# GLA loop of a hybrid diffusion step: early forward output, a buffer for the w_ada blocks, decay two slots ahead, output norm folded into the weights

## The chip, the cores and the metric

The kernel runs on one core of one Trainium2 chip. The metric is the device time of one execution in microseconds (us); lower is better. The engines are PE (TensorE: matmuls; its weight loads are listed apart as PEld), DVE (VectorE), ACT (ScalarE), POOL (GpSimd) and SP (SyncE, which here issues most DMAs).

## The reference

One inference step of two layers on 256 context tokens and 1024 latent tokens with 1024 channels. Layer 0 is gated linear attention (GLA), layer 1 softmax attention. Each layer normalises its input, modulates it with shift and scale vectors that come from `silu(c) @ w_ada + b_ada`, mixes tokens, multiplies by `silu(gate)`, projects with an output matrix and adds the result, times a gate vector, to the input. What matters here is the GLA layer, per head, cut to its core:

```
def step(S, inp):                      # one chunk of tokens
    qe, ke = qi * exp(b), ki * exp(-b)     # b: running sum of the log decay
    a = where(mask, qe @ ke.T, 0)
    o = a @ vi + qe @ S                    # within the chunk + from the state
    S = exp(b_last) * S + (ki * exp(b_last - b)).T @ vi

o_f = scan(forwards);  o_b = scan(backwards)
o = rms_norm(o_f + flip(o_b), onorm)       # per head, 256 values
y = (o * silu(gate)) @ w_out
```

There are 4 heads with 128 key and 256 value channels. The log decay is `log_sigmoid((h @ wa1) @ wa2 + ba) / 16`, one for each direction.

## The kernel before, in words

Matmuls that need more than half precision are made of three: each operand is split into a high and a low half-precision part (`mm3`, L113). Weights are therefore prepared first: `stage` (L129) loads 1 MB into a tile `wst`, of which there are two for everybody, takes the largest absolute value (four reductions, L135) and derives a power of two from it (`pow2`, L72, with a matmul at L77 that spreads the maximum over the partitions). `fill` (L143) then writes the high part with ACT (L150) and the low part with DVE (L151); `split_ahead` (L154) does the same for the attention weights and stores them to memory.

**The GLA loop** (`gla`, L585) has 50 slots: five passes over the ten tiles of 128 tokens. Pass h handles head h in one direction (forwards for even h, backwards for odd h) and, in the same slots, finishes head h-1 in the opposite direction. In before, a slot does this, in program order:

- `combine` (L536) finishes head h-1 on tile i: three products are summed in one PSUM bank (L548): scores times values (`at`, `v`), queries times the state of the first direction (`Sa`), queries times the state of the second direction (`Sc`). ACT sums the squares (L551), DVE and POOL take the root (L107, L109), and DVE multiplies by the row factor and the norm vector `onorm` (L554).
- `decayed` (L456) turns the decay of this slot into `en`, `ep` and so into `ke` and `qe` by a matmul with a triangle matrix (L461) into the bank `cs`.
- `decay` (L434) prepares the decay of the next slot: a matmul into bank `z` (L437), three ACT steps (L442 to L444), DVE (L446, L447), and the split into `ghi` on POOL (L451) and `glo` on DVE (L452).
- `value_gate` (L414) projects value and gate of the tile (the many matmuls of L118) and applies silu to the gate.
- `intra` (L474) transposes the keys into bank `kt` (L479), copies them out (`ks`, L481), makes the scores in bank `A` (L484), masks them (L487) and adds the two directions (`at`, L489).
- `gated` (L557) multiplies output and gate (L559) and stores the tile.
- `filler` (L1153) does work of other stages in fixed slots: in even slots from 4 on, `gemv` (L221) loads a 1 MB block of `w_ada` into a `wst` tile (L227) and multiplies it with the conditioning vectors (16 small matmul instructions, L231); `mod_sum` adds it up a slot later; other slots split weights ahead (`AHEAD`, L39) or fill the output weights (`WO`, L37).
- `outer` (L492) makes the tile's share of the state in bank `U` (L500, L503), ACT copies one half out (`u`, L505), and `scan` (L509) advances the state with DVE (`Wa`, `Wc`, L527) and POOL (`Sa`, `Sc`, L521, L523).

The PSUM has eight banks; in the loop they are two `mm` (projections, `gemv`, `mod_sum`), `z` (decay, and the spreading matmul of `pow2`), `cs`, `A`, `kt`, `U` and `o`.

**The order of the work** isn't written out by hand. The Tile framework is called with a simulated timeline (L44): while the program is built it places each ready instruction on its engine, those earlier in the program first, and adds the waits for tiles and banks. What comes out is one fixed order for each engine and each DMA queue; at run time an instruction that has to wait holds back those behind it.

After the loop `gla_out` multiplies by the output weights (`wo`), and layer 1 follows.

Of the kernel before, what the change touches and what calls it, by code (L numbers as in the profile page):

```python
# [7 lines left out]
F16 = mybir.dt.float16  # L8
F32 = mybir.dt.float32
I32 = mybir.dt.int32  # L10
AF = mybir.ActivationFunctionType
# [36 lines left out]
class K:  # L48
# [92 lines left out]


    def fill(self, w, j, ap):  # L143
# [59 lines left out]
    def cond_vectors(self, rows, brow):  # L203
# [14 lines left out]
        self.modT = [self.t(cp, [P, 16, 2], F32, f"modT{l}") for l in range(2)]  # L218


    def gemv(self, l, b, tag="mm", first=None):  # L221
        nc = self.nc
        src = self.I["w_ada"][l, :, b * 256 : b * 256 + 256].rearrange("(k p) n -> p k n", p=P)
        to = self.t(self.wst, [P, KT, 256], F32, "wst") if first is None else first
        h = KT if first is None else KT // 2
        for j in range(0, KT, h):
            nc.sync.dma_start(to[:, j : j + h], src[:, j : j + h])  # L227
        ps = self.bank(tag)
        for k in range(KT):
            j = k % 4  # L230
            nc.tensor.matmul(  # L231
                ps[32 * j : 32 * j + 32, 0:256], self.cst[:, k, :], to[:, k, :],
                start=k < 4, stop=k >= 4, tile_position=(0, 32 * j), skip_group_check=True,
            )
        m = self.t(self.ew, [P, 256], F32, "mod") if first is None else self.t(self.p1, [P, 256], F32, "mod", bufs=4)
        nc.scalar.copy(m, ps[:, 0:256])
        return l, b, m
# [79 lines left out]
    def gla_consts(self):  # L317
        nc, I = self.nc, self.I
        load = nc.gpsimd.dma_start
        self.ia = self.io = 0  # L320
        self.r = self.t(self.gcp, [98, T], F16, "r")
        self.wa2 = self.t(self.gcp, [98, 2, GQ], F16, "wa2")
        self.cum = self.t(self.gcp, [P, 2, 130], F16, "cum")
        load(self.cum, I["k_cum"])
        self.mask = self.t(self.gcp, [P, 2, P], I32, "mask")
        load(self.mask, I["k_mask"])
        self.onorm = self.t(self.gcp, [P, DV], F32, "onorm")
        load(self.onorm, I["gla_onorm"].to_broadcast([P, DV]))
# [85 lines left out]
    def value_gate(self, h, i, w):  # L414
# [3 lines left out]
        if h < GH:  # L418
            v = self.t(self.tl, [P, DV], F32, f"v{i}")
            self.nc.scalar.activation(v, ps[:, 0:DV], AF.Copy, scale=self.inv_v[h])  # L420
            self.v[h][i] = v
# [12 lines left out]
    def decay(self, h, i):  # L434
# [39 lines left out]
    def intra(self, i, st):  # L474
        nc = self.nc
        ke, qe = st["ke"], st["qe"]
        kt = self.bank("kt")[:, 0 : 2 * P].rearrange("p (d k) -> p d k", d=2)
        for d in range(2):
            nc.tensor.transpose(kt[:, d, :], ke[:, d, :], self.ident)  # L479
        ks = self.t(self.ew, [P, 2, P], F32, "ks")  # L480
        nc.vector.tensor_copy(ks, kt)  # L481
        ap = self.bank("A")[:, 0 : 2 * P].rearrange("p (d k) -> p d k", d=2)
        for d in range(2):
# [3 lines left out]
        nc.vector.copy_predicated(am, self.mask, ap)  # L487
        at = self.t(self.tl, [P, P], F32, f"at{i}")
        nc.gpsimd.tensor_tensor(at, am[:, 0, :], am[:, 1, :], ALU.add)  # L489
# [19 lines left out]
    def scan(self, h, i, d, prev, u, eb, tag):  # L509
        nc = self.nc  # L510
        if prev is None and i < NTP:
# [4 lines left out]
            return None, w  # L516
        s = self.t(self.tl, [P, DV], F32, f"Sa{i}") if tag == "a" else self.t(self.ew, [P, DV], F32, "Sc")
        if prev is None:
# [16 lines left out]

    def combine(self, h, i, c, st, prev):  # L536
        nc = self.nc
        a = 1 - c
        sc, wc = self.scan(h, i, c, prev, st["u"], st["eb"], "c")
        o = self.bank("o" if h < GH - 1 else ("o", "A", "U", "kt")[self.io % 4])[:, 0:DV]  # L540
        self.io += 1
        terms = [(st["at"], self.v[h][i])]
        if st["S"] is not None:
            terms.append((st["qe"][:, a, :], st["S"]))
        if sc is not None:
            terms.append((st["qe"][:, c, :], sc))
        for j, (x, y) in enumerate(terms):
            nc.tensor.matmul(o, x, y, start=j == 0, stop=j == len(terms) - 1)  # L548
        junk = self.t(self.ew, [P, DV], F16, "junk", bufs=1)
        ssq = self.t(self.sm, [P, 1], F32, "ossq")  # L550
        nc.scalar.activation(junk, o, AF.Square, accum_out=ssq)  # L551
        r = self.rstd(ssq, DV, "ors")
        og = self.t(self.ew, [P, DV], F32, "og", bufs=3)
        nc.vector.scalar_tensor_tensor(og, o, r, self.onorm, ALU.mult, ALU.mult)  # L554
        return og, {"W": wc, "eb": st["eb"]}

    def gated(self, h, i, og, g):  # L557
        nc = self.nc
        nc.vector.tensor_tensor(og, og, g, ALU.mult)  # L559
        nc.scalar.dma_start(self.og_d[i, :, h * DV : h * DV + DV], og)  # L560

# [23 lines left out]
    def gla(self, wq, w, filler):  # L585
        asc = list(range(NTP, NT)) + list(range(NTP))
        st = [[None] * NT for _ in range(GH)]
        g = {0: self.decay(0, asc[0])}
        for h in range(GH + 1):
            order = asc if h % 2 == 0 else asc[::-1]  # L590
            a, ends = (0, (NT - 1, NTP - 1)) if h % 2 == 0 else (1, (NTP, 0))
# [6 lines left out]
            for n, i in enumerate(order):  # L598
                slot = h * NT + n
                if i in starts:  # L600
                    prev = cprev = None
                if h > 0:
                    og, cprev = self.combine(h - 1, i, a, st[h - 1][i], cprev)
                if h < GH:
                    s = st[h][i] = self.decayed(h, i, g.pop(slot))
                h2, n2 = divmod(slot + 1, NT)
                if h2 < GH:
                    g[slot + 1] = self.decay(h2, (asc if h2 % 2 == 0 else asc[::-1])[n2])
# [7 lines left out]
                filler(slot)  # L616
                if h < GH:
                    self.outer(h, i, a, s, prev, i in ends)
                    prev = s
                    if i < NTP and i in ends:  # L620
                        self.final_state(h, a, prev)
# [414 lines left out]
def emit(ctx, tc, I, O, dbg=None, stop=None):  # L1036
# [26 lines left out]
    with ExitStack() as c:  # L1063
# [4 lines left out]
        k.ps = k.pool("ps2", 1, PSUM, c)  # L1068
        k.p2_bank = "z"
        banks = ("z", "cs", "A", "kt", "U", "o")  # L1070
        k.gla_init()
        with ExitStack() as c1:
# [24 lines left out]
            for j, b in enumerate((4, 5, 6, 7, 0, 1, 2, 3)):  # L1097
# [8 lines left out]
                to = to.bitcast(F32).rearrange("p (k n) -> p k n", n=256)  # L1106
                parts.append(k.gemv(0, b, ("A", "kt", "U", "o")[j % 4], to))
                if j == 3:
# [41 lines left out]
        queue = [(0, b) for b in (8, 9, 10, 11)] + [(1, b) for b in (4, 5, 6, 7, 0, 1, 2, 3, 8, 9, 10, 11)]  # L1150
        wo, part, prep = [], [], []

        def filler(slot):  # L1153
            if part:
                k.mod_sum([part.pop()])
            if queue and slot >= 4 and slot % 2 == 0:
                part.append(k.gemv(*queue.pop(0)))
            if cols and slot in AHEAD:
                with tc.issue_after(first):
                    k.split_ahead(*cols.pop(0))  # L1160
            if slot in WO:
                b = WO.index(slot)
                if b % 2 == 0:
                    wo.append(k.wtile(b))
                k.fill(wo[-1], b % 2, I["gla_w_out"][0][:, 256 * b : 256 * b + 256])
            if slot == 43:
# [133 lines left out]
```

## Time and profile before

| | us |
|---|---|
| Median of 3 runs | 1375.09 (1372.32 to 1375.16) |
| Profiled execution | 1372.38 |
| its span, first to last instruction | 1370.6 |
| PE busy in the span | 1253.7 |
| DVE busy | 945.3 |
| ACT busy | 653.0 |
| POOL busy | 378.1 |

The GLA loop runs from about 105 to 625 us of the span. A matmul's own duration overlaps that of the next, so the distance between two starts is what it costs PE; the granted PE clock is 1.00 at full speed. In rows of instructions stand the start, the duration, the engine, the line, the operation, the tile written and those read, the shapes, and in square brackets how long the engine stood idle before and what released it. In lists of waits stand the total, the number and the longest.

### The profile page before, as it was taken

To read this page: it belongs to the slowest core of one execution; us is meant where nothing else is said; L and a number is where in the kernel's file an instruction comes from. 1 tells how busy PE (TensorE), PEld (TensorE's weight loads), DVE (VectorE), ACT (ScalarE), POOL (GpSimd) and SP (SyncE) were. 2 spreads that over 40 slices of the span, in tenths; PEclk is the share of its full clock that TensorE was granted. 3 is DMA by queue.
4 is the path that set the end of the run, shared out by engine and by line. 5 is a ranking of instruction groups with operands and counts; after the bars stand their busy time and mean duration, and the time that the engine had idled before them with its cause. 6 is when DMAs were issued, how large, how long until landed. Compare 5 with 4: busy or idle time off the path is not lost. (4 is left out here: it accounts for less than half of the span.)

```text
span 1370.6 us, 21814 instructions
## 1 busy us (share of the span) xinstructions
PE 1253.7 (91%) x7646; PEld 762.0 (56%) x7646; DVE 945.3 (69%) x2148; ACT 653.0 (48%) x1621; POOL 378.1 (28%) x607
## 2 busy tenths in 40 slices
PE   4788899989979998997999998999999989998998
PEld 2346564645545554773444445676765766765443
DVE  2787568765767668876565468888767788875652
ACT  2566345544546445752233356555556455563110
POOL 1233112322311123330122356344335443330000
PEclk9899899999989998998999999999999999999999
DMA  9511545244445435147643446756947666694342
GB/s 324 200 62 43 188 155 170 93 138 143 135 135 185 154 112 168 54 167 212 151 150 108 162 112 139 145 120 142 191 95 166 129 156 139 122 211 139 132 144 93
DMA packets 343486, 198.18 MB, mean 145 GB/s; under 512 B 233598, under 2 KB 331374, under 8 KB 341840
## 3 DMA queue, kind: packets, MB, share of 16 engines
q1 hardware_dynamic: 297312, 158.64, 43.4%
q10 hardware_dynamic: 45728, 37.25, 8.2%
q0 software_dynamic: 336, 0.90, 0.3%
q8 instruction: 60, 0.98, 0.3%
q14 instruction: 50, 0.41, 0.1%
HBM read 103.39 MB, written 37.24 MB: 103 GB/s over the span
## 5 line engine op out<-in xcount | busy, mean ns | idle before, releaser
L118 PE MATMUL mm<-whi,hT_hi 128*128 128x512 f16 (+1 forms) x560 | 198.0, 354 | 0.6 <-ACT gx L918 0.6
L118 PE MATMUL mm<-wlo,hT_hi 128*128 128x512 f16 (+1 forms) x560 | 197.6, 353 | 0.0
L118 PE MATMUL mm<-whi,hT_lo 128*128 128x512 f16 (+1 forms) x560 | 197.1, 352 | 0.0
L118 PEld LDWEIGHTS <-hT_hi 128*128 128x128 f16 x1280 | 125.6, 99 | 111.9 <-issue 6.9
L118 PEld LDWEIGHTS <-whi 128*128 128x128 f16 x1328 | 132.2, 100 | 92.3 <-issue 21.9
L118 PE MATMUL mm<-hT_hi,whi 128*128 128x256 f16 (+1 forms) x512 | 156.8, 309 | 3.5 <-POOL hT_hi L313 2.9
L906 POOL TENSOR_SCALAR phi<-p,srec 128x1280 f16<-128x1280 f32 (+1 forms) x80 | 106.1, 1326 | 191.9 <-DVE srec L901 179.9
L118 PE MATMUL mm<-hT_lo,whi 128*128 128x256 f16 (+1 forms) x512 | 157.0, 307 | 0.4 <-DVE hT_lo L314 0.4
L118 PE MATMUL mm<-hT_hi,wlo 128*128 128x256 f16 (+1 forms) x512 | 156.9, 307 | 0.0
L907 DVE SCALAR_TENSOR_TENSOR plo<-p,srec,phi 128x1280 f16<-128x1280 f32 (+1 forms) x80 | 106.8, 1335 | 40.0 <-POOL phi L906 34.2
L891 PE MATMUL S<-kTh,wst 128*128 128x512 f16 (+1 forms) x416 | 114.4, 338 | 4.2 <-ACT p L899 2.1
L894 DVE TENSOR_REDUCE smx<-S 128x1 f32<-128x1280 f32 (+1 forms) x80 | 101.2, 1267 | 8.6 <-PE S L891 8.6
L118 PE MATMUL mm<-PTh,vh 128*128 128x256 f16 x336 | 91.8, 273 | 13.0 <-DMA PTh<-phi 12.4
L899 ACT ACTIVATE p<-S,snb,sexp 128x1280 f32<-128x1280 f32 (+1 forms) x80 | 99.3, 1241 | 4.2 <-ACT snb L896 0.4
L118 PE MATMUL mm<-PTl,vh 128*128 128x256 f16 x336 | 91.8, 273 | 7.5 <-DMA PTl<-plo 7.4
L118 PEld LDWEIGHTS <-hT_lo 128*128 128x128 f16 x640 | 63.1, 99 | 60.9 <-DVE hT_lo L314 3.1
L135 DVE TENSOR_REDUCE wmx<-wst 128x1 f32<-128x512 f32 x120 | 74.5, 676 | 30.5 <-DMA wst<-in_att_w_in 13.4
L118 PE MATMUL mm<-PTh,vl 128*128 128x256 f16 x336 | 91.9, 273 | 0.0
L891 PEld LDWEIGHTS <-wst 128*128 128x128 f16 x624 | 61.0, 98 | 54.4 <-issue 3.0
L118 PEld LDWEIGHTS <-wlo 128*128 128x128 f16 x640 | 63.6, 99 | 37.2 <-issue 4.7
L118 PEld LDWEIGHTS <-vh 128*128 128x128 f16 x672 | 65.8, 98 | 26.7 <-issue 9.1
L891 PE MATMUL S<-kTl,wst 128*128 128x512 f16 (+1 forms) x208 | 70.3, 338 | 0.0
(336 smaller groups left out, 2712.3 us busy)
## 6 DMA issues: line engine op xcount, KB each, us to landing
wst<-in_w_ada SPq DMA_DIRECT2D x16, 1024.0 KB, 5.9
wst<-in_gla_w_in SPq DMA_DIRECT2D x12, 1024.0 KB
wst<-in_att_w_in SPq DMA_DIRECT2D x10, 1024.0 KB, 6.3
og_d<-og ACTq DMA_DIRECT2D x80, 128.0 KB, 2.1
x_d<-xr ACTq DMA_DIRECT2D x10, 512.0 KB, 5.2
wst<-og_d SPq DMA_DIRECT2D x5, 1024.0 KB, 4.9
xr<-x_d SPq DMA_DIRECT2D x10, 512.0 KB, 6.8
out<-xr ACTq DMA_DIRECT2D x10, 512.0 KB, 2.6
```

Of the source, the lines that this page charges most:

```text
L118: self.nc.tensor.matmul(out, a, b, start=k == 0 and j == 0, stop=k == n - 1 and j == 2)
L135: nc.vector.tensor_reduce(mx[:, j : j + 1], st[:, 2 * j : 2 * j + 2, :], AX.XY, ALU.max, apply_absolute_value=True)
L891: nc.tensor.matmul(S[:, a : a + n], x, y, start=m == 0, stop=m == 2)
L894: nc.vector.tensor_reduce(mx, S, AX.X, ALU.max)
L899: nc.scalar.activation(p, S, AF.Exp, scale=self.sexp, bias=nb, accum_out=den)
L906: nc.gpsimd.tensor_scalar(hi, p, r, 2.0 ** 14, ALU.mult, ALU.mult)
L907: nc.vector.scalar_tensor_tensor(lo, p, r2, hi, ALU.mult, ALU.subtract)
```

## The change

Five edits, all in the GLA loop.

- **Forward output early.** `combine` is split. `local` runs in the slot after the tile's own first pass: it sums the first two products in one half of bank `o`, and ACT copies them to a tile `oa`. `combine`, a pass later, makes only the third product, in the other half of the bank, and DVE adds `oa`. The tiles `v`, `at` and `Sa`, one for each token tile before, are now two in turn. `combine` also moves from the head of the slot to behind `intra`.
- **Banks.** `kt` and `A` become the halves of one bank `kA`; the bank that this frees, `p2`, takes the spreading matmul of `pow2`, which was in `z`.
- **w_ada blocks.** The load (`ada_load`) is called in odd slots from 1 on, into a buffer of its own; the matmuls (`gemv`) in the even slot after it.
- **Decay** is called two slots ahead rather than one; `ghi` and `glo` get three buffers each.
- **Norm in the weights.** `onorm` is multiplied into the rows of `gla_w_out` while these are split (`fill_out` in place of `fill`); `gated` multiplies output, row factor and gate in one instruction.

The diff, cut to its core:

```diff
+    def fill_out(self, w, j, ap):
+        nc = self.nc
+        st = self.t(self.wst, [P, KT, 256], F32, "wst")
+        nc.sync.dma_start(st, ap.rearrange("(k p) n -> p k n", p=P))
...
+        o2 = self.onorm.unsqueeze(1).to_broadcast([P, 2, 2])
+        nc.vector.tensor_tensor(mx, mx, o2, ALU.mult)
+        m = self.t(self.small, [P, 1], F32, "wm1")
+        nc.vector.tensor_reduce(m, mx, AX.XY, ALU.max, apply_absolute_value=True)
+        s, w[2][j] = self.pow2(m)
+        so = self.t(self.small, [P, 2], F32, "wso")
+        nc.vector.tensor_scalar(so, self.onorm, s, None, ALU.mult)
...
+                nc.scalar.activation(hi, par[:, q, :, b, :], AF.Copy, scale=so[:, b : b + 1])
+                nc.vector.scalar_tensor_tensor(lo, par[:, q, :, b, :], so[:, b : b + 1], hi, ALU.mult, ALU.subtract)
...
+    def ada_load(self, l, b, to, h=KT):
         src = self.I["w_ada"][l, :, b * 256 : b * 256 + 256].rearrange("(k p) n -> p k n", p=P)
-        to = self.t(self.wst, [P, KT, 256], F32, "wst") if first is None else first
...
+            self.nc.sync.dma_start(to[:, j : j + h], src[:, j : j + h])
+        return l, b, to
...
-            v = self.t(self.tl, [P, DV], F32, f"v{i}")
+            v = self.t(self.tl, [P, DV], F32, "v", bufs=2)
...
-        hi = self.t(self.ew, [P, 2, DK], F16, "ghi")
-        lo = self.t(self.ew, [P, 2, DK], F16, "glo")
+        hi = self.t(self.tl, [P, 2, DK], F16, "ghi", bufs=3)
+        lo = self.t(self.tl, [P, 2, DK], F16, "glo", bufs=3)
...
-        kt = self.bank("kt")[:, 0 : 2 * P].rearrange("p (d k) -> p d k", d=2)
+        ka = self.bank("kA").rearrange("p (j d k) -> p j d k", j=2, d=2)
+        kt, ap = ka[:, 0], ka[:, 1]
...
-    def combine(self, h, i, c, st, prev):
...
+    def local(self, h, i, a, st):
+        nc = self.nc
+        both = self.bank("o").rearrange("p (j n) -> p j n", j=2)
         terms = [(st["at"], self.v[h][i])]
         if st["S"] is not None:
             terms.append((st["qe"][:, a, :], st["S"]))
+        for j, (x, y) in enumerate(terms):
+            nc.tensor.matmul(both[:, 0], x, y, start=j == 0, stop=j == len(terms) - 1)
+        st["oa"] = self.t(self.tl, [P, DV], F32, f"oa{i}")
+        nc.scalar.copy(st["oa"], both[:, 0])
+        return both[:, 1]
+
+    def combine(self, h, i, c, st, prev, o):
+        nc = self.nc
+        sc, wc = self.scan(h, i, c, prev, st["u"], st["eb"], "c")
+        og = st["oa"]
         if sc is not None:
...
+            nc.tensor.matmul(o, st["qe"][:, c, :], sc, start=True, stop=True)
+            og = self.t(self.ew, [P, DV], F32, "og", bufs=3)
+            nc.vector.tensor_tensor(og, o, st["oa"], ALU.add)
...
+        nc.scalar.activation(junk, og, AF.Square, accum_out=ssq)
+        return og, self.rstd(ssq, DV, "ors"), {"W": wc, "eb": st["eb"]}
...
+    def gated(self, h, i, og, r, g):
+        nc = self.nc
+        nc.vector.scalar_tensor_tensor(g, og, r, g, ALU.mult, ALU.mult)
+        nc.scalar.dma_start(self.og_d[i, :, h * DV : h * DV + DV], g)
...
-                if h > 0:
-                    og, cprev = self.combine(h - 1, i, a, st[h - 1][i], cprev)
                 if h < GH:
                     s = st[h][i] = self.decayed(h, i, g.pop(slot))
-                h2, n2 = divmod(slot + 1, NT)
+                h2, n2 = divmod(slot + 2, NT)
...
                 x = self.value_gate(h, i, w)
                 if h < GH:
                     self.intra(i, s)
+                o = self.local(*local) if local else None
                 if h > 0:
-                    self.gated(h - 1, i, og, x)
+                    og, r, cprev = self.combine(h - 1, i, a, st[h - 1][i], cprev, o)
+                    self.gated(h - 1, i, og, r, x)
...
-        k.p2_bank = "z"
-        banks = ("z", "cs", "A", "kt", "U", "o")
+        k.p2_bank = "p2"
+        banks = ("z", "cs", "kA", "p2", "U", "o")
...
+        k.ada = k.pool("ada", ctx=c)
...
-            if queue and slot >= 4 and slot % 2 == 0:
-                part.append(k.gemv(*queue.pop(0)))
+            if slot % 2 == 0:
+                if held:
+                    part.append(k.gemv(*held.pop()))
+            elif queue:
+                held.append(k.ada_load(*queue.pop(0), k.t(k.ada, [P, KT, 256], F32, "wada")))
```

More of the change, by code (lines that the diff above doesn't have):

```diff
@@ L218, in cond_vectors, with gemv @@
         self.modT = [self.t(cp, [P, 16, 2], F32, f"modT{l}") for l in range(2)]
-    def gemv(self, l, b, tag="mm", first=None):
-        nc = self.nc
-        src = self.I["w_ada"][l, :, b * 256 : b * 256 + 256].rearrange("(k p) n -> p k n", p=P)
-        to = self.t(self.wst, [P, KT, 256], F32, "wst") if first is None else first
-        h = KT if first is None else KT // 2
-        for j in range(0, KT, h):
-            nc.sync.dma_start(to[:, j : j + h], src[:, j : j + h])
+    def ada_load(self, l, b, to, h=KT):
+        src = self.I["w_ada"][l, :, b * 256 : b * 256 + 256].rearrange("(k p) n -> p k n", p=P)
+        for j in range(0, KT, h):
+            self.nc.sync.dma_start(to[:, j : j + h], src[:, j : j + h])
+        return l, b, to
+    def gemv(self, l, b, to, tag="mm", first=False):
+        nc = self.nc
         ps = self.bank(tag)
@@ L234, in gemv @@
             )
-        m = self.t(self.ew, [P, 256], F32, "mod") if first is None else self.t(self.p1, [P, 256], F32, "mod", bufs=4)
+        m = self.t(self.p1, [P, 256], F32, "mod", bufs=4) if first else self.t(self.ew, [P, 256], F32, "mod")
         nc.scalar.copy(m, ps[:, 0:256])
@@ L326, in gla_consts @@
         load(self.mask, I["k_mask"])
-        self.onorm = self.t(self.gcp, [P, DV], F32, "onorm")
-        load(self.onorm, I["gla_onorm"].to_broadcast([P, DV]))
+        self.onorm = self.t(self.gcp, [P, 2], F32, "onorm")
+        load(self.onorm, I["gla_onorm"].rearrange("l (j p) -> p (l j)", p=P))
         self.sum3 = self.t(self.gcp, [96, 96], F32, "sum3")
@@ L516, in scan @@
             return None, w
-        s = self.t(self.tl, [P, DV], F32, f"Sa{i}") if tag == "a" else self.t(self.ew, [P, DV], F32, "Sc")
+        s = self.t(self.tl, [P, DV], F32, "S" + tag, bufs=2)
         if prev is None:
@@ L586, in gla @@
         asc = list(range(NTP, NT)) + list(range(NTP))
+        orders = [asc if h % 2 == 0 else asc[::-1] for h in range(GH + 1)]
         st = [[None] * NT for _ in range(GH)]
-        g = {0: self.decay(0, asc[0])}
+        g = {n: self.decay(0, asc[n]) for n in range(2)}
+        local = None
         for h in range(GH + 1):
-            order = asc if h % 2 == 0 else asc[::-1]
+            order = orders[h]
             a, ends = (0, (NT - 1, NTP - 1)) if h % 2 == 0 else (1, (NTP, 0))
@@ L1150, in emit @@
         queue = [(0, b) for b in (8, 9, 10, 11)] + [(1, b) for b in (4, 5, 6, 7, 0, 1, 2, 3, 8, 9, 10, 11)]
-        wo, part, prep = [], [], []
+        wo, part, prep, held = [], [], [], []
         def filler(slot):
```

41 lines of the change are left out of this document (20 added, 21 removed).

## The prediction

> **What bounds the kernel now.** I read the page first (PE is busy 91% of the span), then cut the GLA loop into six stretches with the view of windows; the first is its first pass over the ten tiles. Its columns are the stretch in us, its length, busy time with number of instructions of PE, PE's weight loads, DVE, ACT and POOL, the granted PE clock, the DMA share and GB/s.
>
> ```profile
> 105.00:196.00 91.00, 79.11 (x584) 54.76 (x583) 62.82 (x165) 44.26 (x101) 19.46 (x40) 0.92 0.40 128
> 196.00:301.00 105.00, 96.11 (x565) 58.29 (x564) 76.14 (x207) 54.51 (x144) 27.18 (x49) 0.95 0.42 137
> 301.00:398.00 97.00, 89.16 (x483) 50.02 (x483) 69.33 (x185) 50.98 (x134) 26.42 (x47) 0.95 0.49 150
> 398.00:497.00 99.00, 98.87 (x573) 55.73 (x572) 65.49 (x173) 52.50 (x133) 17.29 (x35) 1.00 0.47 145
> 497.00:594.00 97.00, 86.63 (x462) 56.77 (x461) 78.19 (x213) 53.62 (x145) 32.04 (x53) 0.89 0.31 107
> 594.00:625.00 31.00, 30.63 (x215) 22.47 (x214) 22.11 (x60) 18.79 (x52) 5.57 (x9) 1.00 0.75 221
> sum 520.00, PE 480.51 PEld 298.05 DVE 374.07 ACT 274.67 POOL 127.95; mean PE 80.09 PEld 49.67 DVE 62.34 ACT 45.78 POOL 21.32
> ```
>
> PE bounds the loop: it idles 520 - 480.5 = 39.5 us, DVE idles 146. One stretch of 99 us (398 to 497) has next to no idle time and a clock of 1.00, so the loop can run dense; the loss sits elsewhere. The waits of PE between 105 and 628 us name it (total us, times, longest).
>
> ```profile
> PE mm L231 <- DMA wst<-in_w_ada: 14.2, 5, 7.6
> PE cs L461 <- POOL ghi L451: 7.5, 4, 2.5
> PE A L484 <- DVE orsa L107: 2.8, 1, 2.8
> PE z L437 <- DVE g L446: 2.6, 1, 2.6
> PE kt L479 <- DVE en L467: 2.5, 2, 2.3
> PE o L548 <- DVE og L554: 2.2, 2, 1.3
> PE U L500 <- ACT v L420: 2.1, 3, 0.9
> PE z L437 <- DVE orsa L107: 1.3, 1, 1.3
> PE U L548 <- DVE og L554: 1.3, 1, 1.3
> PE cs L461 <- DVE glo L452: 0.4, 2, 0.2
> ```
>
> Nearly all of it lies in seven stretches, and there the clock falls too:
>
> ```profile
> 128.00:143.00 15.00, 7.83 (x42) 3.58 (x41) 9.77 (x24) 7.80 (x18) 3.57 (x7) 0.66 0.65 201
> 158.00:171.00 13.00, 9.06 (x70) 6.23 (x68) 7.08 (x15) 6.65 (x16) 1.26 (x3) 0.87 0.73 232
> 230.00:242.00 12.00, 9.49 (x43) 5.02 (x41) 10.11 (x26) 4.44 (x14) 5.79 (x9) 0.86 0.63 207
> 272.00:290.00 18.00, 12.71 (x60) 6.42 (x59) 14.15 (x35) 9.75 (x25) 5.73 (x9) 0.81 0.67 220
> 380.00:399.00 19.00, 11.15 (x51) 5.37 (x51) 14.51 (x38) 9.56 (x25) 5.29 (x9) 0.73 0.74 231
> 497.00:508.00 11.00, 8.22 (x31) 5.08 (x30) 8.88 (x23) 2.45 (x8) 4.10 (x7) 0.69 0.42 146
> 512.00:537.00 25.00, 18.73 (x77) 11.37 (x76) 19.97 (x55) 13.64 (x36) 8.54 (x12) 0.73 0.50 165
> ```
>
> Idle time in them is the sum of length less PE, 113 - 77.2 = 35.8 us. What a low clock does, the same 16 matmuls of a w_ada block show, once behind dense work and once behind the longest wait:
>
> ```profile
> 341.47 1.07 PE L231 MATMUL mm<-wst,cst 128*32 128x256 f32 x16
> 385.53 0.37 SPq L227 DMA_DIRECT2D wst<-in_w_ada  x1
> 392.35 1.93 PE L231 MATMUL mm<-wst,cst 128*32 128x256 f32 x16 [7.57 <-DMA wst<-in_w_ada]
> ```
>
> They take 1.07 us or 1.93 us: about half speed. If a lowered clock is half the clock, the time at it is 2 x the sum of (1 - clock) x length: 2 x (5.10 + 1.69 + 1.68 + 3.42 + 5.13 + 3.41 + 6.75) = 54.4 us. If all 35.8 us of idle time fall into it, 18.6 us of work ran at half speed and lost 9.3 us; if none does, 27.2 us. I take 17, near the middle. So at most 39.5 + 17 = 56 us are to be had in the loop, a time of 1316 us.
>
> [...]
>
> **w_ada blocks.** In the trace the 1 MB load starts at 385.53 and PE, which has nothing else in its order ahead of the block, stands until 392.35: the load and its use are one call, and the buffer, one of two, is shared with every weight that is split. The edit gives the block its own buffer, loads it a slot earlier, and takes 16 loads out of the shared one. The view of the load's line gives the time to landing (min/median/max):
>
> ```profile
> DMA to landing us min/median/max: 5.4/7.8/9.8
> ```
>
> A slot is 520/50 = 10.4 us in the mean, so the lead covers the median and mostly the maximum. Queued on SP is the same number of loads; a load held by a buffer holds those behind it, and that gets rarer. I take 12 of the 14.2 us. Between: all 14.2, and nothing if SP's queue holds the load as long as before. With the shared buffers freer, the splitting loads start earlier as well; I count nothing for that.
>
> **Decay two slots early.** It removes PE's wait for ghi and glo, 7.5 + 0.4 us: its chain (ACT three times, DVE twice, POOL, DVE) then has a slot more. I take 7. It adds no instruction. The z matmul still needs the one z bank, but the scale search (L77) gets a bank of its own: of the z waits, 2.6 + 1.3 = 3.9, I take half, 2.
>
> **Forward output early.** The matmuls are the same: two of the three terms move from the next pass into the slot after their own tile. From the timeline of the last pass, a term (two instructions) costs PE 0.44 us from start to start:
>
> ```profile
> 607.78 0.60 PE L548 MATMUL kt<-v,at 128*128 128x256 f32 x2
> 608.22 0.59 PE L548 MATMUL kt<-Sc,qe 128*128 128x256 f32 x2
> ```
>
> So about 20 x 0.44 = 9 us leave the last pass and enter the first, which has 91 - 79.1 = 12 us of idle time; I count 0 for the exchange, with -5 and +5 as ends. Added: 40 copies of the finished half on ACT, 36 adds on DVE; gone: the multiply by the norm, since the product with the gate takes the row factor along. By groups:
>
> ```profile
> L505 ACT COPY u<-U 128x256 f32<-128x256 f32 x36 | 13.3, 369 | 18.7 <-PE U L503 11.8 <-DVE p2m L81 2.2 <-PE mm L118 2.1
> L554 DVE SCALAR_TENSOR_TENSOR og<-o,ors,onorm 128x256 f32<-128x256 f32 x32 | 15.3, 478 | 2.0 <-POOL ors L109 1.9
> L559 DVE TENSOR_TENSOR og<-og,gx 128x256 f32<-128x256 f32 x40 | 17.2, 432 | 0.5
> L527 DVE TENSOR_TENSOR Wa<-Sa,U 128x256 f32<-128x256 f32 x32 | 13.2, 413 | 6.1 <-ACT u L505 6.1
> ```
>
> ACT gets 40 x 0.37 = 15 us on 275 of 520; DVE loses 40 x 0.478 and gains 36 x 0.413, some 4 us less. Both lie beside PE. The waits for og (2.2 + 1.3 us) go, since the bank is free after one add instead of after square, root and multiply: 3.5. What is late next is the first term of the bank's new order: the copy on ACT.
>
> **Banks shared.** This is the new cost. kt and A become halves of one bank, and so do the two halves of the output. The last row above shows that halves of a bank are not read independently: Wa reads one half of U, u the other, neither needs the other's data, and yet Wa waited 6.1 us for u. So A's matmuls now wait until ks has been copied out of kt, and the cross term until the copy on ACT is done: 40 + 36 = 76 handovers. How late ks can be:
>
> ```profile
> 340.71 0.38 PE L479 MATMUL kt<-ident,en 128*128 128x128 f32 x2
> 340.93 0.61 PE L484 MATMUL A<-qe,en 128*128 128x128 f32 x4
> 343.65 0.42 DVE L481 COPY ks<-kt 128x256 f32<-128x256 f32 x1
> ...
> 350.16 0.42 PE L479 MATMUL kt<-ident,en 128*128 128x128 f32 x2
> 350.41 0.61 PE L484 MATMUL A<-qe,en 128*128 128x128 f32 x4
> 350.61 0.42 DVE L481 COPY ks<-kt 128x256 f32<-128x256 f32 x1 [0.75 <-PE kt L479]
> ```
>
> The copy ends 3.4 us and 0.9 us behind kt's start, where A followed after 0.2. If PE had nothing to run meanwhile, 76 x 0.9 = 68 us were lost; if the order fixed at build time finds other matmuls (the projection's 24 per tile are mostly independent), nothing. The nearest rows are banks reused today: z with 40 decays, 3.9 us of waits, and o with 40 outputs, 3.5 us: about 0.09 us each. I take 76 x 0.08 = 6 us. Queued behind a waiting A are all later matmuls, and behind these everyone.
>
> [...]
>
> **Norm in the weights.** Four fills get three small DVE instructions more, about 0.15 us each: 2 us beside PE, 0 in the sum.
>
> **The sum**, on the profiled execution's 1372.4 us: waits -12 - 7 - 2 - 3.5 = -24.5. Of the slow-clock loss the same share goes, 24.5/39.5 x 17 = -10.5. Handovers +6. Together -29, 1343. The median of the runs is 2.7 us above that execution, so I forecast **1344**. The stretch behind 625 us is left alone; it holds waits of its own that a shifted start can move by a few us either way.
>
> **Rivals.**
> *Only the load is cured* (1361): the order on each engine is fixed at build time, and a chain that is ready earlier may be put earlier, with as little slack as before. For it: five of seven stretches hold DVE at over 70% busy, and DVE is what was late. Against: ghi's slack grows by a whole slot. -12, -5 for the clock, +6 = -11.
> *The shared banks pace the slot* (1398, slower): A behind ks, the cross term behind ACT's copy, on every tile. The gains are 35 us, so it decides from 35/76 = 0.46 us a handover. At 0.8, just below the shorter lag above, it is 61 - 35 = +26. For it: DVE starts ks up to 3 us late; against: U needs ks today as well, and PE waited for it at no place of the list above.
> *The waits move* (1372): as many us of new waits as old ones go, since the planned order drifts from the chip's.
>
> **How the numbers follow.** Forecast 0.50, with its own range 1318 to 1366; only the load 0.13; banks 0.30; waits move 0.07. A change of 0.2%, some 2.7 us, is about what a measurement can tell from none. Faster: 0.50 + 0.13 = 0.63; same 0.07; slower 0.30. The range goes from 1315, the loop without idle time, to 1395, which takes in nearly half of the bank rival and leaves out under 0.2.
>
> **What would show it.** PE's waits for in_w_ada and ghi gone from the list; the clock at 0.95 or more in the first five of the stretches; the last pass shorter by about 9 us and the first not longer. Against it: PE waiting at A for ks, or at the cross term for oa, in tens of us; SP issuing the w_ada load only shortly before its block.

## The result, and the profile after

The changed kernel takes 1393.43 us in the median (1388.14 to 1395.79, 4 runs), beside 1374.01 us for the kernel before on the same chip (1372.32 to 1375.16, 4 runs): 1.0136 times as long, 95% interval 1.0117 to 1.0155. I had forecast 1344, faster than before; it is 19 us slower than before. The time lies inside the range, on the wrong side of no change.

The first lines of the page of after: the same number of matmuls and nearly the same PE time as before (1253.7), in a longer span (1370.6 before).

```profile
span 1392.4 us, 21826 instructions
...
PE 1257.1 (90%) x7646; PEld 762.3 (55%) x7646; DVE 943.1 (68%) x2152; ACT 663.4 (48%) x1661; POOL 383.8 (28%) x607
```

The view of windows, over the stretches of the prediction; only the last one is drawn out to 645, since the loop's last store now starts at 642 us instead of 625.7. Columns as in the prediction: stretch, length, busy time of PE, weight loads, DVE, ACT, POOL, granted clock, DMA share, GB/s.

```profile
105.00:196.00 91.00, 83.78 (x627) 59.44 (x626) 70.43 (x183) 50.90 (x122) 21.95 (x40) 0.98 0.55 174
196.00:301.00 105.00, 97.98 (x576) 58.24 (x575) 74.96 (x207) 57.01 (x145) 23.82 (x41) 0.97 0.49 156
301.00:398.00 97.00, 82.25 (x423) 45.19 (x422) 71.85 (x191) 48.75 (x123) 21.15 (x36) 0.91 0.52 160
398.00:497.00 99.00, 93.66 (x541) 53.86 (x539) 66.19 (x178) 52.63 (x143) 26.30 (x44) 1.00 0.38 121
497.00:594.00 97.00, 85.41 (x468) 51.63 (x467) 60.67 (x162) 49.68 (x146) 27.41 (x51) 1.00 0.16 53
594.00:645.00 51.00, 40.09 (x267) 28.57 (x266) 29.45 (x83) 25.52 (x73) 11.29 (x20) 0.97 0.51 151
```

The clock is higher than before in three of the six (0.98 for 0.92, 0.97 for 0.95, 1.00 for 0.89) and lower in two (0.91 for 0.95, 0.97 for 1.00), and yet the loop is 16 us longer: PE idles 56.8 us of these 540, 39.5 of 520 before, in shorter pieces. The other 5 us of the longer span lie behind the loop's last store (750.2 us, 744.9 before); d2_norm, below, bears on them. The list of PE's waits in the loop of after (105 to 645 us; total, times, longest) shows what took the place of the old ones.

```profile
PE mm L118 <- ACT gx L451: 11.1, 7, 3.0
PE kA L507 <- DVE am L514: 8.0, 8, 2.9
PE cs L488 <- ACT ep L492: 4.8, 5, 1.7
PE kA L511 <- DVE qe L496: 4.5, 3, 2.6
PE mm L276 <- ACT gx L451: 3.8, 1, 3.8
PE mm L118 <- ACT q L432: 3.8, 1, 3.8
PE o L570 <- POOL at L516: 3.6, 6, 1.1
PE kA L511 <- DVE ks L509: 2.7, 3, 1.9
```

The waits for `in_w_ada` (14.2 us before) and for `ghi` and `glo` (7.9) are gone, as forecast. New are above all three kinds: projections behind ACT's `gx`, the shared bank `kA` from both sides, and the early product (L570) behind POOL's scores. The longest single wait fell from 7.6 to 3.8 us, and the clock rose while the idle time grew. The longest waits alone don't account for the clock, though: half clock also follows a shorter one. In after PE is busy 1.57 us between 622.0 and 626.6, with one wait of 3.03, and the view of windows gives a clock of 1.00 there and 0.50 from 626.6 to 630.0. ACT's waits in the loop of after name what is behind the first and the third kind.

```profile
ACT v L447 <- PE o L570: 31.0, 15, 5.2
...
ACT gx L451 <- DMA og_d<-gx: 21.9, 11, 4.1
```

The output is now stored from the gate's own tile `gx`, of which there are two, and no longer from `og`, of which there are three. ACT can't write the next gate until the store has landed: it waits 21.9 us for that, 4.1 at the longest. And ACT's next value `v` (two in turn now) waits until the early product has read the older one: 31.0 us, where before ACT's `v` waited 10.9 us for products into `o`. Eight microseconds from the timeline of after show both and the bank in one chain:

```profile
579.87 0.68 PE L511 MATMUL kA<-qe,en 128*128 128x128 f32 x4
...
582.27 0.43 DVE L514 COPY_PREDICATED am<-mask,kA 128x256 f32<-128x256 int32 x1
...
582.75 0.44 PE L507 MATMUL kA<-ident,en 128*128 128x128 f32 x2 [2.21 <-DVE am L514]
582.97 0.69 POOL L516 TENSOR_TENSOR at<-am 128x128 f32<-128x128 f32 x1
...
583.71 0.70 PE L570 MATMUL o<-v,at 128*128 128x256 f32 x2 [0.52 <-POOL at L516]
...
584.45 0.47 ACT L447 ACTIVATE v<-mm,inv_v 128x256 f32<-128x256 f32 x1 [2.21 <-PE o L570]
...
587.27 0.47 ACT L451 ACTIVATE gx<-mm,inv_g 128x256 f32<-128x256 f32 x1 [2.02 <-DMA og_d<-gx]
587.80 0.27 PE L118 MATMUL mm<-whi,hT_hi 128*128 128x256 f16 x1 [1.66 <-ACT gx L451]
```

DVE masks the scores 1.7 us after they are made; the next tile's transposes, in the other half of the bank, wait 2.21 us for that; the early product waits for POOL; ACT's `v` waits 2.21 us for the product, `gx` 2.02 us for a store, and PE 1.66 us for `gx`.

### The profile page after: what moved, and what is told of

It is laid out like the page before. It is cut to its first block, busy times and chain, and to the rows that moved or that the text cites. A ratio compares the mean times of both kernels' runs of the same rounds, so it can differ in the third digit from the quotient of the medians.

```text
span 1392.4 us, 21826 instructions
## 1 busy us (share of the span) xinstructions
PE 1257.1 (90%) x7646; PEld 762.3 (55%) x7646; DVE 943.1 (68%) x2152; ACT 663.4 (48%) x1661; POOL 383.8 (28%) x607
## 3 DMA queue, kind: packets, MB, share of 16 engines
q1 hardware_dynamic: 297312, 158.64, 45.7%
## 5 line engine op out<-in xcount | busy, mean ns | idle before, releaser
L135 DVE TENSOR_REDUCE wmx<-wst 128x1 f32<-128x512 f32 x104 | 64.7, 677 | 34.0 <-DMA wst<-in_gla_w_in 15.1
```

The source lines that it names most:

```text
L135: nc.vector.tensor_reduce(mx[:, j : j + 1], st[:, 2 * j : 2 * j + 2, :], AX.XY, ALU.max, apply_absolute_value=True)
```

## The experiments

Each run is a ratio to the kernel before, taken beside it on the same chip; 0.001 of it is 1.4 us. Each interval is some 0.002 to 0.004 to either side, so a difference of two ratios is good to some 4 to 8 us.

### The store and the bank

**a1_gx4**: the changed kernel with four gate tiles.

```diff
-            x = self.t(self.ew, [P, DV], F32, "gx")
+            x = self.t(self.ew, [P, DV], F32, "gx", bufs=4)
```

> Changed kernel, but the gate tile gx has four buffers rather than two. Store theory (the output is now stored from gx, so ACT's next write of gx waits for the store to land, 21.9 us on ACT, and PE behind it 11.1 + 3.8 + 0.7 = 15.6 us): these waits go, and the time falls by about 16 us to 1378 (1370 to 1384). Bank theory (the shared banks pace the slot): no more than 3 us, 1390 or more. Order theory (every edit makes another fixed order, and new waits take the place of old ones): the waits for gx go, but the time stays within 5 us of 1393.

1400.71 us, ratio 1.019 (1.0154 to 1.0227): not faster. PE's waits for `gx` fell to 4.4 us and others grew (`kA` behind `am` 9.3, `z` behind `g` 4.9). The store alone is not the cause.

**a2_banks**: the changed kernel with `kt` and `A` in banks of their own and `pow2`'s matmul back in `z`.

```diff
-        ka = self.bank("kA").rearrange("p (j d k) -> p j d k", j=2, d=2)
-        kt, ap = ka[:, 0], ka[:, 1]
+        kt = self.bank("kt")[:, 0 : 2 * P].rearrange("p (d k) -> p d k", d=2)
+        ap = self.bank("A")[:, 0 : 2 * P].rearrange("p (d k) -> p d k", d=2)
```

> Changed kernel, but keys transposed (kt) and scores (A) have banks of their own again, and the spreading matmul of the scale search goes back into bank z. Bank theory: PE's waits at kA for am, ks and wm (8.0 + 2.7 + 2.4 + 0.4 us) go and some 3 us come back at z, so about 10 us faster, 1383. Store theory: the 15.6 us behind gx stay, 1388 or more. Order theory: within 5 us of 1393.

1388.58 us, 1.0087 (1.006 to 1.0115): some 7 us of the 19, less than the 10 of the bank theory.

**a3_both**: both edits.

> Changed kernel with four gx buffers and with kt and A in banks of their own (both edits at once). Store and bank theory together: 26 us off, 1367, below the kernel before. Store theory alone: as with the buffers alone, 1378. Order theory: 1385 or more.

1380.83 us, 1.0034 (1.0005 to 1.0063). Both together take 14 us back, about half of the 26 that the store and the bank theory expected together. With the banks apart the gate tiles bring 7 us (a2_banks to a3_both), and with four gate tiles the banks bring 21 (a1_gx4 to a3_both), so what each is worth depends on the other. It is still not faster than the kernel before, though the waits for `in_w_ada`, `ghi` and `glo` are gone, those of the shared bank nearly, and those for `gx` down to 1.7 us. What is left at the head of PE's list in a3_both:

```profile
PE o L570 <- POOL at L516: 11.0, 7, 3.2
PE A L511 <- DVE qe L496: 4.9, 5, 1.8
PE U L527 <- ACT v L447: 4.7, 2, 2.7
```

**b1_store**: the kernel before, with the product written into `gx` and stored from there, and nothing else.

```diff
-        nc.vector.tensor_tensor(og, og, g, ALU.mult)
-        nc.scalar.dma_start(self.og_d[i, :, h * DV : h * DV + DV], og)
+        nc.vector.tensor_tensor(g, og, g, ALU.mult)
+        nc.scalar.dma_start(self.og_d[i, :, h * DV : h * DV + DV], g)
```

> Kernel before, with one edit: the product of output and gate is written into the gate tile gx (two buffers) and stored from there, rather than from og (three buffers). Store theory: ACT waits for the stores at gx by some 20 us as in the changed kernel, PE behind it, 8 to 16 us slower, 1382 to 1390. Bank theory: no change, within 3 us of 1374. Order theory: any time within 10 us, without waits for the store on ACT's list.

1380.79 us, 1.0036 (1.002 to 1.0052): the store by itself costs 5 us, less than the 8 to 16 that I expected. ACT waits 9.2 us for stores at `gx`, and the largest new wait of PE stands behind it:

```profile
PE mm L118 <- ACT gx L424: 6.0, 1, 6.0
```

### The place of the early products

**c1_late**: a3_both with `local` called at the end of the slot. (In the first slot of a pass it still comes ahead of `combine`, which needs it.)

```diff
-                o = self.local(*local) if local else None
...
                 filler(slot)
                 if h < GH:
                     self.outer(h, i, a, s, prev, i in ends)
+                if local:
+                    self.local(*local)
```

Its two products have bank `o` to themselves, and `combine`'s product takes the next use of that bank.

> The kernel with four gx buffers and banks apart, in which the first two output terms of a tile are called at the end of the next slot rather than in its middle, and write the bank on their own. Chain theory (made right behind its own pass, the output waits at PE for the scores, 11.0 us at L570): that wait goes, and the time falls by 8 to 11 us below that kernel's 1381, to some 1371. Order theory (another fixed order, other waits of the same total): that wait goes or not, the time stays within 5 us of 1381.

1357.54 us, 0.9887 (0.9856 to 0.9919): 20 us less than a3_both, twice what I expected, and faster than the kernel before. PE's list in c1_late has no wait for `at` left:

```profile
PE mm L118 <- ACT gx L451: 6.4, 4, 3.2
PE y L118 <- DMA whi<-wst: 4.9, 2, 2.6
PE U L527 <- DVE ks L509: 3.9, 2, 2.7
PE A L511 <- DVE qe L496: 3.7, 2, 3.4
```

I measured in each trace how long after the end of a POOL row `at` the next product on `v` and `at` starts. In after 16 of 40 start within 0.5 us, the median is 1.1 us; in a3_both 14 and 1.8; in c1_late none, and 7.3. Then ACT waits much less for the products, too. In the view of the tile `at`, under who waited for it, a3_both and c1_late have:

```profile
  ACT v L447: 26.8, 14
```
```profile
  ACT v L447: 5.6, 3
```

**g1_split** tells the place from the bank: the products have bank `o` to themselves as in c1_late, but are called where the change put them.

> a3_both with the early products at the place that the change gave them (called behind intra), but no longer in one half of a bank with combine's product in the other: they take the whole of bank o, and combine takes the next use of it, as in c1_late. Against c1_late only the place of the call differs. Place theory: nothing is gained, 1374 to 1384, and PE's waits for at stay at about 10 us. Theory of the shared halves: most of the 23 us between a3_both and c1_late is gained, 1357 to 1366.

1379.71 us, 1.0028 (1.0004 to 1.0051), and PE waits 10.3 us for `at`. The shared halves of `o` are worth next to nothing (1.0034 in a3_both); the place is worth 19 us (0.9887 in c1_late).

**l1_late**: the changed kernel itself with `local` late; bank `kA` and two gate tiles as they are.

> The changed kernel with one thing moved: the call of local goes from behind intra to behind outer, at the end of the same slot, and its product has the whole of bank o, combine's product the bank after it. The shared bank kA, two gx buffers, the w_ada buffer, the decay lead and the norm stay as in the changed kernel. Place theory (the early products stand high in program order, so the build-time order puts them on PE just when its timeline has the scores ready, and on the chip POOL is later): most of the loss goes, 1366 to 1375 us, PE's waits for at gone, the waits at kA (13 us before) and for gx (about 15 us) left. Bank and store theory (the early products' place matters little while kA and gx hold PE): 1385 to 1393.

1373.18 us, 0.9986 (0.9961 to 1.001): 21 us less than after. The products also have the whole of bank `o` here, which g1_split showed to be worth next to nothing, so this is the place again. ACT's wait of `v` for the products falls from 31.0 us in after to 7.2, and PE's for `at` from 3.6 to 1.0.

**l2_late_gx4**: l1_late with four gate tiles.

> l1_late with four gx buffers: the changed kernel with the early products late and the store free, but kt and A still in one bank. Against l1_late only the gx buffers differ, against c1_late only the bank. Bank theory (kt's transposes wait for the mask to have read A, A's matmuls for ks): 1368 to 1375, waits at kA of 10 to 15 us. Store theory: 1357 to 1363, the waits for gx gone and little in their place.

1369.97 us, 0.9963 (0.9945 to 0.9981). The gate tiles bring 3 us, which is inside the uncertainty; from here to c1_late, where only the bank differs, it is 10 us. Its list still has the waits of the shared bank, the first and the third row here:

```profile
PE kA L507 <- DVE am L514: 5.4, 5, 1.8
PE kA L511 <- DVE qe L496: 3.0, 2, 2.3
PE kA L511 <- DVE ks L509: 2.5, 2, 2.0
```

### The load and the decay lead

**e2_noada**: a3_both with the `w_ada` blocks loaded in the slot of their use, into `wst`, as before.

```diff
-            if slot % 2 == 0:
-                if held:
-                    part.append(k.gemv(*held.pop()))
-            elif queue:
-                held.append(k.ada_load(*queue.pop(0), k.t(k.ada, [P, KT, 256], F32, "wada")))
+            if queue and slot >= 4 and slot % 2 == 0:
+                part.append(k.gemv(*k.ada_load(*queue.pop(0), k.t(k.wst, [P, KT, 256], F32, "wst"))))
```

> The kernel with four gx buffers and banks apart, with the w_ada blocks loaded as before the change (shared buffer, load and use in one call, from slot 4). Load theory (the buffer of its own removes 14 us of waits and the slow clock behind them): these waits return and it is 12 to 20 us slower than 1381, 1393 to 1401. Order theory: the waits for the load return, others go, within 5 us of 1381.

1377.48 us, 1.0035 (0.9999 to 1.0072): the same as a3_both. With the early products in their early place the load's own buffer is worth nothing, although 6.6 us of waits for `in_w_ada` are back.

**c3_late_noada**: the same edit on c1_late.

> c1_late with the w_ada blocks loaded as before the change: in the slot of their use, into the shared wst buffers. Load theory (now that PE has few other waits, the wait for the block is not hidden by anything): 1365 to 1372, with 7 to 14 us of waits for in_w_ada. Rival, from the same edit on a3_both (no difference): 1354 to 1361.

1373.7 us, 0.9983 (0.9964 to 1.0003): now the buffer is worth 13 us, and without it the old wait is back at the head of the list:

```profile
PE mm L258 <- DMA wst<-in_w_ada: 11.1, 4, 5.6
```

**c2_late_decay1**: c1_late with the decay one slot ahead (and two buffers each for `ghi` and `glo`).

```diff
-                h2, n2 = divmod(slot + 2, NT)
+                h2, n2 = divmod(slot + 1, NT)
```

> c1_late with the decay one slot ahead again, as in the kernel before. Decay theory (the lead of two slots removes PE's waits for ghi and glo, 8 us, and their share of slow clock): 1366 to 1370, with these waits back in the list. Rival, from the run of the decay lead alone (10 us slower than before): the lead itself costs, and without it the time is 1345 to 1355.

1358.72 us, 0.9871 (0.9832 to 0.9909): no difference. Beside the other edits the lead is worth nothing, and PE waits 2.3 us for `ghi` and not 7.5. Neither of my two expectations held.

**c4_late_only**: c1_late without the buffer and without the lead.

> c1_late with both the w_ada blocks and the decay as before the change; what is left is the early output in its late place, the norm in the weights and four gx buffers. If the early output in its late place is what gains, 1354 to 1362. If it gains only together with the load and the decay lead, since each of them leaves PE a wait at another place, 1368 to 1378, about the time of the kernel before.

1382.79 us, 1.005 (1.0026 to 1.0073): 7 us above the kernel before, and above both times that I had expected. Some 7 us come with the norm's new tile, which this kernel has too (d2_norm, below). So the early output without the two, in its late place, gains nothing. From here the buffer brings 25 us (to c2_late_decay1) and the lead 9 (to c3_late_noada), but both together 22 (to c1_late): as if they cured the same stalls, and the buffer is enough.

**d1_decay**: the kernel before with the lead and the norm in the weights.

> Kernel before with two parts of the change only: the decay two slots ahead, and the norm in the weights (output still stored from og). Decay theory: the waits for ghi and glo (7.9 us) go with some of the slow clock, 1366 (1360 to 1370). Order theory: these waits go, but the time stays within 5 us of 1375.

1384.27 us, 1.0085 (1.0063 to 1.0107): 12 us slower, above both times that I had expected; d2_norm, below, has 7 of them without the lead. The wait for `ghi` only falls from 7.5 to 5.8 us, and another one grows from 2.5 to 10.0:

```profile
PE mm L257 <- DMA wst<-in_w_ada: 15.3, 6, 5.6
PE kt L505 <- DVE en L493: 10.0, 2, 5.4
PE cs L487 <- POOL ghi L477: 5.8, 5, 2.8
```

### The order of combine, and the norm

**p1_order**: the kernel before with `combine` behind `intra`.

> Kernel before with one move and nothing else: the call of combine stands behind intra rather than at the head of the slot, as in the change. Same instructions, same banks, same buffers. Order theory: the fixed order alone moves the time by 5 us or more, either way, with PE's waits in other places. Store and bank theories: none of their mechanisms is touched, within 4 us of 1375.

1376.99 us, 1.0033 (1.0008 to 1.0059): some 4 us slower, a little less than the 5 of the order theory and no clear answer.

**c5_head**: c1_late with `combine` back at the head of the slot.

> c1_late with combine back at the head of the slot, where it stood before the change. Order theory (combine moved behind intra cost 3 us in the kernel before, since what it feeds comes later): 1351 to 1356. Rival (what stands higher in program order is placed on PE as soon as it looks ready, so the third product at the head waits for Sc and oa on the chip): 1360 to 1368, with PE's waits for Sc and oa up from 3 us.

1355.1 us, 0.987 (0.9846 to 0.9894): 2 us less than c1_late, inside the uncertainty. The move costs 4 us alone, and here no cost is shown.

**d2_norm**: the kernel before with the norm in the weights alone.

> The kernel before with onorm multiplied into the rows of gla_w_out alone (fill_out for fill, the row factor by itself in combine). Against d1_decay only the decay lead is missing. If the norm was costed rightly at nothing, 1373 to 1378, and the 10 us of d1_decay are the lead's. If the norm costs, 1381 to 1386, by DVE's three added small instructions or by the weights' chain of splitting, and the lead costs nothing.

1382.65 us, 1.0048 (1.0026 to 1.007): 7 us for an edit that I had costed at nothing. The loop's last store starts at 623.7 us, 2 us earlier than before; the loss comes behind it, in layer 1, which the edit doesn't touch. There the transposes by DMA take longer to land. The rows of the list of DMAs (bytes and number unchanged; the last figure is the median us to landing) and of queue 1's share, first before, then d2_norm:

```profile
q1 hardware_dynamic: 297312, 158.64, 43.4%
...
PTh<-phi SPq DMA_TRANSPOSE x80, 3.0
PTl<-plo SPq DMA_TRANSPOSE x80, 3.1
```
```profile
q1 hardware_dynamic: 297312, 158.64, 46.3%
...
PTh<-phi SPq DMA_TRANSPOSE x80, 3.6
PTl<-plo SPq DMA_TRANSPOSE x80, 3.5
```

`fill_out` adds a small tile `wso` (six buffers, 192 bytes of each partition) to a pool that lies below the tiles of layer 1. In the built programs `PTh` lies at byte 128512 before and at 128704 in d2_norm and in after.

**d3_norm_place**: d2_norm with that tile in another pool. The order of instructions is the same on every engine.

```diff
-        so = self.t(self.small, [P, 2], F32, "wso")
+        so = self.t(self.sm, [P, 2], F32, "wso", bufs=6)
```

> d2_norm with one thing changed: the small tile wso comes from the pool sm2 on the other side of the memory, so that the tiles of layer 1 lie at the addresses of the kernel before again (PTh at byte 128512 of the partition, not 128704). The order of instructions is the same on every engine. Address theory: the DMA transposes land in 3.0 us again, PE's waits for PTh and PTl fall from 25 to 20 us, and the time is 1373 to 1377. Rival (the norm's own instructions or the order that they bring cost the 7 us): 1380 to 1385.

1375.03 us, 0.9986 (0.9962 to 1.001), and in the list of d3_norm_place:

```profile
q1 hardware_dynamic: 297312, 158.64, 43.6%
...
PTh<-phi SPq DMA_TRANSPOSE x80, 3.0
PTl<-plo SPq DMA_TRANSPOSE x80, 3.1
```

So the norm's instructions do cost nothing, and the 7 us came with the addresses. The part behind the loop's last store is 754.2 us in d2_norm, 747.1 here and 744.9 before. PE's waits for `PTh` and `PTl` fell less than I expected, from 25.4 to 23.3 us (19.8 before); which waits carry the rest I haven't separated. What the shift does inside a transfer no trace shows, and no other shift was tried.

**c6_head_place**: c5_head with the same line changed, the version with the lowest ratio.

> c5_head with the same one change, wso in the pool sm2. Address theory: the part behind the loop gets 5 to 8 us shorter, 1347 to 1350 us, the transposes land in 3.0 to 3.2 us (3.8 in c5_head). Rival: 1353 to 1357.

1354.35 us (1346.61 to 1356.26, 6 runs), ratio 0.9816 (0.9772 to 0.9859): faster than both kernels. Its transposes land in 3.1 and 3.4 us, where c5_head has 3.8 for both. What that is worth here is not settled: 7 us by the ratios, whose intervals overlap, 3 by the spans of the two traces (1357.7 and 1354.3), 1 by the medians, and the median lies in the range of the rival.

## Why the prediction was wrong

From c6_head_place to after leads a chain of runs that differ by one thing each. In ratios times 1375 us, each good to 4 to 7, so that the +2 and the +3 are not told from nothing:

| from, to | what comes in | us |
|---|---|---|
| before, c6_head_place | the change without the five items below | -25 |
| c6_head_place, c5_head | the 192 bytes (1 to 7) | +7 |
| c5_head, c1_late | `combine` behind `intra` | +2 |
| c1_late, l2_late_gx4 | `kt` and `A` in one bank | +10 |
| l2_late_gx4, l1_late | two gate tiles | +3 |
| l1_late, after | early products called behind `intra` (and in half of bank `o`) | +21 |

The parts also depend on the order in which they are taken: the bank is worth 7 us, 10 or 21, by the kernel that it is tested on, and four gate tiles anything from 7 lost (a1_gx4) to 7 gained.

Without the 6 us of handovers I had summed a gain of 35 us; 20 to 25 are measured in c6_head_place, which has `kt` and `A` apart, and all of it comes with the buffer for the load (c4_late_only has none, c2_late_decay1 has it without the lead). The buffer alone on the kernel before was not run. Step by step:

**w_ada blocks** (-12, and their part of the clock, -5): right in kind, all 14.2 us of waits went, and worth 13 to 25 us where the early products stood late. Where they stood early it was worth nothing (a3_both and e2_noada are equal), PE standing elsewhere in its stead. The 7.8 us that I took for the load's landing mixes in sixteen half blocks loaded ahead of the loop; the sixteen in the loop landed in 5.4 to 6.4 us (median 5.9), so a slot covers them with more to spare.

**Decay two slots early** (-7, z -2): the waits went, those at `z` (3.9 us) too, but as a gain this step failed too. Beside the buffer the lead is worth nothing (c2_late_decay1), and on the kernel before most of the wait for `ghi` stayed and a longer one came at `kt` (d1_decay). For this step the rival "only the load is cured" was right.

**Forward output early** is the step that failed. I "count 0 for the exchange, with -5 and +5 as ends"; it cost 21 us. The exchange itself went the way forecast only in part: from ACT's last `v` of the loop to the last store it took 54.4 us before, 46.8 in a3_both, 43.3 in c1_late and 51.3 in c6_head_place, but 57.8 in after, and 51.8 in d3_norm_place, which has no exchange at all. The waits for `og` fell, from 3.5 to 0.5 us, and what I named as late next, "the copy on ACT", was not it: PE waits 0.9 us for it in after. The products became consumers of `at`, the end of the chain from A through DVE's mask to POOL, in the next slot, where before they read it a pass later. On the chip 16 of 40 products started within 0.5 us of `at`, which is how a product starts that PE stood waiting for (0.05 us behind it in the chain above). That the builder's timeline had `at` ready sooner than the chip is how I explain it; the timeline itself wasn't compared. PE's own waits for `at` are 3.6 us in after. With two `v` tiles in place of ten, the delay went on to ACT (31.0 us). My own sentence, that a chain ready earlier "may be put earlier, with as little slack as before", I applied to the decay and not to this. That it is the place is shown by c1_late against g1_split and by l1_late against after; that the loss spreads through `v` is read from the waits, which fall with it (31.0 to 7.2 us), and more tiles of `v` and `at` were not tried.

**Banks shared** (+6): it is 10 us in the chain above, so the term was too small; and the handover I priced, A behind `ks`, is the small one (2.7 us of waits). The dear one is the other way round: the next tile's transposes behind the mask that reads A (8.0 us). I listed 40 handovers at this bank where there are two for each tile, 80. At some 0.13 us each it stays far below the 0.46 from which the bank rival decides. The other 36, between the halves of `o`, are worth next to nothing (g1_split), and that rival is not the cause by itself.

**The store.** I overlooked that `gated` now stores from `gx`, two tiles, instead of `og`, three. The prediction lists this instruction only as one multiply fewer. It costs 5 us alone (b1_store), 7 with the banks apart (a2_banks to a3_both) and 3, inside the uncertainty, late in the chain above; curing it alone gained nothing (a1_gx4).

**Norm in the weights** (0): right for the instructions (the three small ones on DVE took 0.17, 0.14 and 0.24 us each in after, in the median), wrong by 7 us for the tile that it adds.

**Slow clock** (-10.5): the clock did rise, from 0.965 to 0.978 over the span, though not to 0.95 in every stretch as I had named for a sign. I took it as a share of the idle time that goes; here the longest waits went and the idle time grew, so the two don't move together.

What c1_late and c2_late_decay1 leave open is why the lead helps without the buffer and not with it; and the order that the builder finds changes as a whole with every edit, so single waits can't be added up across runs.

## What to carry to other kernels

When an edit brings a consumer nearer to its producer, cost the lost distance first: on engines with an order fixed at build time, work placed as soon as a timeline believes it ready may have no slack on the chip (16 of 40 products in after started within 0.5 us of `at`), and the cure may be one call moved to the end of the stage (20 us in c1_late). Count buffers by what holds them longest: a tile that becomes the source of a store is held until the store lands (21.9 us of ACT's waits in after), and two halves of one bank are handed over both ways for each tile (8.0 and 2.7 us of PE's waits there). A gain that is real can be worth nothing until the next stall is gone, so test parts also on top of the cured kernel, and not on the old one alone.

## What the runs showed of the hardware

I hadn't expected that 192 bytes of shift, with the same order on every engine, slow 160 transposes by DMA from some 3.0 to 3.6 us and the kernel by some 7 us, in a stage that the edit doesn't touch. It shows only in the times to landing and in the queue's share (43.4% to 46.3%): packets and bytes are the same to the last digit. The share tells the two apart in other kernels, too: it is 45.7% to 46.8% in after, c1_late, c5_head and d2_norm, which have the tile in that pool, and 42.9% to 44.0% in the five without it there (before, p1_order, b1_store, d3_norm_place and c6_head_place).
